# Regrouping the columns of the modulations' weight pieces: four 128-column matmuls a piece

## The chip, the cores and the metric

The kernel runs on one core of one Trainium2 chip. The metric is the device time of one execution in microseconds, taken as the median of several runs. Beside the times there is one profiled execution of the kernel before; its page and its trace are what the numbers below are read from.

## The reference

The program is two transformer-like blocks in float32, with 256 latent tokens, 256 context tokens and 1024 features. The first block has two layers; each layer's input is modulated by a shift, a scale and a gate that come from a condition vector, once for the latents (`c`) and once for the context (`c_ctx`):

```python
cond = jax.nn.silu(c)
cond_ctx = jax.nn.silu(c_ctx)
for i in range(DEPTH):
    sh, sc, gt = jnp.split(cond @ w_mod[i] + b_mod[i], 3, axis=-1)
    sh_c, sc_c, gt_c = jnp.split(cond_ctx @ w_mod[i] + b_mod[i], 3, axis=-1)
    h_lat = x * (1.0 + sc[:, None]) + sh[:, None]
    h_ctx = ctx * (1.0 + sc_c) + sh_c
    ...
    x = _layernorm(DEEPNORM_ALPHA * x + gt[:, None] * y_lat, ln_g[i], ln_b[i])
```

`w_mod[i]` is 1024 x 3072. Layer 0 is an attention with 16 heads (MLA), layer 1 a state space mixer (S5). The second block has a pooling and gating mixer, a cross attention and a feed-forward part. The products `cond @ w_mod[i]` and `cond_ctx @ w_mod[i]` are what the change is about.

## The kernel before

TensorE multiplies the transposed weights of a piece with activations that stand with features on the partitions. Most products are written as three matmuls of rounded parts (L119, L120, L121: high by high, high by low, low by high). The modulations are different: the condition, only two columns wide and padded to 32 (`self.cs`), is the stationary operand, and the raw float32 weights are the moving one. Such a matmul fills 32 of the array's 128 columns, one of its four column groups, and writes 32 partitions of the bank `modps`. A float32 matmul leaves two records in the trace, so four records are two matmuls.

Layer 0's shift and scale are computed at the very start (`start`, L678): four matmuls of 128 columns in the four column groups, for eight chunks of features, four rounds from each 1 MB piece. The rest goes through `mod` (from L577): layer 0's gate (part 1, 1024 columns), then layer 1's shift and scale (part 0, 2048 columns) and its gate (part 1). Each part has 1024 rows in eight chunks `kc`, and pieces `mraw` of 512 columns (256 KB, two buffers), loaded by SyncE at L588. The bank's partitions 32 j to 32 j + 31 hold the j-th quarter of the part's columns: `w` is 512 columns for part 0 and 256 for part 1. So a piece of part 0 is one matmul of 512 columns in one group, and a piece of part 1 two matmuls of 256 columns in two groups. There are 16 + 32 + 16 = 64 pieces. After a part ScalarE copies the bank out (L596), TensorE turns it (L601), and VectorE adds the bias (L604).

`mod` is a generator. Each call of `side` takes one step of it, a piece or an end, and some steps of the S5 operators' preparation (`s5_prep`: sp_t, sp_r, sp_o on VectorE, rtps and gps on TensorE). `side` is called once after each of 16 gate chunks (`mla_in`) and three times in each of the 18 rounds of the heads' pipeline (`mla_heads`): after the value projection of two heads back (uv), after the next head's `values` (pv), and after `queries` (qabs), ahead of `turn` (ptl, ptc). What is left is run before layer 0's norm (`ln_mod`).

TensorE keeps the order in which the code is written. On VectorE, ScalarE and SyncE a scheduler decides, by its own estimate of when things are ready; so a change in TensorE's work can shift the order on these engines, too. SyncE's queue is strict: a reload of `mraw` that waits for a buffer holds up what stands behind it.

Of the kernel before, what the change touches and what calls it, by code (L numbers as in the profile page):

```python
# [11 lines left out]
F32 = mybir.dt.float32  # L12
# [16 lines left out]
class InOrder:  # L29
    """An engine whose instructions go through net.in_order."""  # L30
# [9 lines left out]
class Net:  # L40
# [16 lines left out]
    def phase(self, wts, **banks):  # L57
        """A phase's weight pieces (raw and as parts: numbers of buffers) and its share-out of PSUM's eight banks."""
# [9 lines left out]
    def pinned(self, *engines):  # L68
        """Instructions of these engines, too, keep the order that they are written in."""
# [5 lines left out]
    @contextmanager  # L75
    def behind(self, level=1):
        """What is written in this context fills the gaps of what is written outside."""
        self.tc.cur_priority += 1000000 * level
        yield
        self.tc.cur_priority -= 1000000 * level  # L80
# [7 lines left out]
    def weight(self, src, keep=None):  # L88
        """A weight piece [128, 1024] from DRAM as its parts (high, low); keep: a pool, a name and a number of
        buffers for those that are used more than once."""  # L90
# [20 lines left out]
    def in_order(self, ins):  # L111
        """Keeps an instruction behind those that are written before it, where its engine is in self.ordered."""
# [3 lines left out]
    def mm(self, out, a, b, start, stop):  # L116
        """out += a.T @ b, with a and b given as (high, low)."""
# [6 lines left out]
    def rms_open(self, n, nk, feats, tp, bufs=2, tag="ps", cut=0):  # L124
        """Sums up the squares of nk chunks [128, n], over the chunks first and then over the partitions: one column
        of the bank per 128 tokens. Chunk cut starts a second sum over chunks."""
# [13 lines left out]
    def rms_sum(self, r):  # L140
        """The sum over the partitions, of every n-th column."""
# [7 lines left out]
    def rsqrt(self, s, y, scale, tp):  # L149
        """y = 1 / sqrt(s * scale + eps): the exponent's half, negated, and three Newton steps."""  # L150
# [9 lines left out]
    def rms_close(self, r, between=None, tag="ps"):  # L160
        """1 / sqrt(mean + eps) of each token, on every partition [128, n], in PSUM."""
# [23 lines left out]
    def s5_lambda(self, lam, pool, tp):  # L185
        """Powers of lambda-bar, the input coefficient and the scan's multipliers, from lam and log_dt; in steps."""
        nc, v = self.nc, InOrder(self, self.nc.vector)
        n = 128
# [56 lines left out]
        # powers: [128, re/im, dir*pair, 9]  # L245
# [26 lines left out]
        # (lambda-bar - 1) / lam  # L272
# [17 lines left out]
        # powers 1..8, and 0..7 times that coefficient: per direction and piece (re, re + im, im - re) of [j, power]  # L290
# [1495 lines left out]
```

## Time and profile before

| | |
|---|---|
| median of three runs | 1501.27 us (1500.88 to 1508.71) |
| span of the profiled execution, first to last instruction | 1494.4 us |
| TensorE busy | 1379.3 us, 92% |
| VectorE busy | 1152.3 us, 77% |
| ScalarE busy | 712.5 us, 48% |

The profiled execution's own time is its span of 1494.4 us and what lies around it. The page does not give the latter; the median of the runs is 6.9 us above the span. A piece's matmuls overlap with their neighbours, and the ends of matmuls are modelled, so the distance from one start to the next says more than a record's own duration.

### The profile page before, as it was taken

The numbers are of one execution on the slowest core, as the hardware profiler recorded it, in microseconds if no ns is written. First come the engines' busy times: TensorE is split into PE (matmuls) and PEld (weight loads), VectorE is DVE, ScalarE is ACT, GpSimd is POOL, SyncE is SP. The second block draws the span as 40 slices with busy tenths as digits, with TensorE's granted clock in tenths as the row PEclk, the third lists the DMA queues.
The fourth block names the chain that finished last, engine by engine and source line by source line (L and its number), as shares of the span: only waits on it lengthen the run. The fifth ranks groups of instructions, "written<-read, shape, count | busy, mean of one in ns | idle before, by whom it ended". The sixth has DMA issues, their size and how long they took to land.

```text
span 1494.4 us, 30436 instructions
## 1 busy us (share of the span) xinstructions
PE 1379.3 (92%) x12192; PEld 1201.1 (80%) x12192; DVE 1152.3 (77%) x2122; ACT 712.5 (48%) x1307; POOL 100.5 (7%) x221
## 2 busy tenths in 40 slices
PE   5889979999999998898877779999998999999997
PEld 4657656667777778798866669999998999999996
DVE  7989886787768779839988966755568876788887
ACT  4434435655555544622244244544447556565554
POOL 0012211110011011001111000000000000000000
PEclk9989988999999999999988989999999999999999
DMA  9459984454435444578787676555555544445552
GB/s 359 160 170 319 297 247 127 141 156 143 140 120 156 149 131 139 174 223 282 276 294 281 246 266 212 194 194 198 184 183 164 171 169 141 158 171 192 187 184 99
DMA packets 140622, 291.35 MB, mean 195 GB/s; under 512 B 30480, under 2 KB 70080, under 8 KB 135104
## 3 DMA queue, kind: packets, MB, share of 16 engines
q1 hardware_dynamic: 108592, 232.01, 45.5%
q0 software_dynamic: 11360, 49.34, 10.4%
q10 hardware_dynamic: 20528, 8.06, 2.0%
q8 instruction: 95, 1.56, 0.4%
q14 instruction: 47, 0.39, 0.1%
HBM read 234.83 MB, written 54.53 MB: 194 GB/s over the span
## 4 chain that ended last, share of the span: by engine, by line
PE 69%; DVE 15%; issue 7%; DMA 6%; ACT 2%; POOL 0%; SPq 0%; DVEq 0%; ACTq 0%; POOLq 0%
PE lin L119 14%; PE lin L120 14%; PE lin L121 13%; PE modps L591 3%; DVE s_t L493 3%; DVE wl L98 2%; DMA sp_x<-in_s_bcw_dram 2%; PE slat L119 2%; DMA d_o<-sp_o 1%; PE sctx L119 1%; PE dn L121 1%; PE dn L119 1%; PE dn L120 1%; DVE s_V L495 1%; DVE sp_t L37 1%
## 5 line engine op out<-in xcount | busy, mean ns | idle before, releaser
L97 ACT CAST wh<-wr 128x1024 fp32r<-128x1024 f32 x268 | 280.5, 1048 | 407.2 <-PE lin L120 250.0
L98 DVE TENSOR_TENSOR wl<-wr,wh 128x1024 fp32r<-128x1024 f32 x268 | 327.5, 1223 | 148.2 <-ACT wh L97 147.7
L119 PE MATMUL lin<-prH,wh 128*128 128x256 f32 x512 | 145.3, 284 | 0.0
L119 PE MATMUL lin<-yaH,wh 128*128 128x256 f32 x512 | 144.8, 283 | 0.0
L120 PE MATMUL lin<-yaL,wh 128*128 128x256 f32 x512 | 144.6, 282 | 0.0
L121 PE MATMUL lin<-prH,wl 128*128 128x256 f32 x512 | 143.7, 281 | 1.0 <-DVE wl L98 1.0
L121 PE MATMUL lin<-yaH,wl 128*128 128x256 f32 x512 | 144.1, 281 | 0.0
L120 PE MATMUL lin<-prL,wh 128*128 128x256 f32 x512 | 143.8, 281 | 0.2 <-DVE prL L109 0.2
L120 PEld LDWEIGHTS lin<-prL,wh 128*128 128x128 f32 x512 | 96.7, 189 | 1.7 <-DVE prL L109 0.6
L119 PEld LDWEIGHTS lin<-yaH,wh 128*128 128x128 f32 x512 | 97.5, 190 | 0.0
L119 PEld LDWEIGHTS lin<-prH,wh 128*128 128x128 f32 x512 | 96.7, 189 | 1.0
L121 PEld LDWEIGHTS lin<-yaH,wl 128*128 128x128 f32 x512 | 97.4, 190 | 0.0
L120 PEld LDWEIGHTS lin<-yaL,wh 128*128 128x128 f32 x512 | 97.3, 190 | 0.0
L121 PEld LDWEIGHTS lin<-prH,wl 128*128 128x128 f32 x512 | 96.3, 188 | 1.2 <-DVE wl L98 1.2
L493 DVE TENSOR_TENSOR s_t<-s_V,s_tab 128x256 f32<-128x256 f32 (+2 forms) x120 | 73.2, 652 | 15.7 <-ACT s_V L475 14.5
L121 PE MATMUL u<-h,wl 128*128 128x256 f32 x224 | 66.0, 295 | 9.3 <-DVE wl L98 9.3
L427 POOL DMA_DIRECT2D d_t<-sp_g x128 | 66.8, 529 | 56.9 <-DVE sp_g L37 52.6
L121 PE MATMUL lin<-h,wl 128*128 128x256 f32 x128 | 42.4, 331 | 29.7 <-DVE wl L98 29.7
L119 PE MATMUL u<-h,wh 128*128 128x256 f32 x224 | 66.1, 295 | 0.0
L120 PE MATMUL u<-h,wh 128*128 128x256 f32 x224 | 65.6, 293 | 0.5 <-issue 0.5
L119 PE MATMUL lin<-hH,wh 128*128 128x512 f32 x144 | 60.6, 421 | 0.7 <-ACT hH L103 0.7
L37 DVE TENSOR_TENSOR sp_t<-s_pb,sp_x 128x1024 f32<-128x1024 f32 x64 | 60.0, 952 | 0.6
(481 smaller groups left out, 3871.8 us busy)
## 6 DMA issues: line engine op xcount, KB each, us to landing
wr<-in_glu_dram SPq DMA_DIRECT2D x64, 512.0 KB, 3.3
wr<-in_w_up_dram SPq DMA_DIRECT2D x44, 512.0 KB, 4.2
wr<-in_w_in_dram SPq DMA_DIRECT2D x32, 512.0 KB, 4.8
mraw<-in_w_mod_dram SPq DMA_DIRECT2D x64, 256.0 KB, 3.1
d_rt<-sp_rt SPq DMA_DIRECT2D x64, 256.0 KB, 4.0
d_o<-sp_o SPq DMA_DIRECT2D x32, 512.0 KB, 4.8
wr<-in_s_in_dram SPq DMA_DIRECT2D x32, 512.0 KB, 4.5
s_op<-d_o POOLq DMA_DIRECT2D x16, 1024.0 KB, 7.9
```

What stands on the lines that cost most here:

```text
L37: return lambda *a, **k: self.net.in_order(f(*a, **k))
L97: self.in_order(nc.scalar.copy(hi, raw))
L98: self.in_order(nc.vector.tensor_tensor(lo, raw, hi.bitcast(F32), SUB))
L119: self.in_order(t.matmul(out, a[0], b[0], start=start, stop=False))
L120: self.in_order(t.matmul(out, a[0], b[1], start=False, stop=False))
L121: self.in_order(t.matmul(out, a[1], b[0], start=False, stop=stop))
L427: nc.gpsimd.dma_start(self.d_t[k].rearrange("s i j e c -> i s j e c")[:, :, j, e], a)
L493: go(v.tensor_tensor(t[:, x], src.to_broadcast([128, 2, 32, n]), a[x].unsqueeze(1).to_broadcast([128, 2, 32, n]), MUL))
L495: go(v.tensor_tensor(dst, dst, t[:, 0], ADD))
L591: self.in_order(nc.tensor.matmul(p[32 * j:32 * j + 32, :w], self.cs[:, kc, :], raw[:, jj * w:jj * w + w], start=(kc == 0), stop=(kc == 7), ...
```

## The change

The host lays each part's weights out as [kc, q, 128 rows, 4 groups, 128 columns]. Piece q of a chunk then holds 128 columns of each of the four quarters, as one contiguous stretch of 256 KB, and its four matmuls of 128 columns go to the four column groups, at columns 128 q of the bank. The number of pieces, their size, the bank's final content, and the steps between which `side` divides the work stay. The clearing flag is now given with the first piece of a part alone (`kc` 0 and `q` 0), once for each group, and the last flag with the last piece. The copy for the start of layer 0 is made from the same array on the host. Comments and docstrings are dropped, too, which changes nothing in the program.

```diff
-    def mod(self, i, parts, m, tp, piece=512, bufs=2):
+    def mod(self, i, parts, m, tp):
         nc = self.nc
         for part in parts:
             src = self.I[f"w_mod{i}_{part}"]
-            w = 512 if part == 0 else 256
+            n = src.shape[1]
             p = self.ps("modps")
             for kc in range(8):
-                for q in range(4 * w // piece):
-                    raw = tp.tile([128, piece], F32, name="mraw", bufs=bufs)
-                    nc.sync.dma_start(raw, src[kc, :, q * piece:q * piece + piece])
-                    for jj in range(piece // w):
-                        j = q * (piece // w) + jj
+                for q in range(n):
+                    raw = tp.tile([128, 4, 128], F32, name="mraw", bufs=2)
+                    nc.sync.dma_start(raw, src[kc, q])
+                    for j in range(4):
                         self.in_order(nc.tensor.matmul(
-                            p[32 * j:32 * j + 32, :w], self.cs[:, kc, :], raw[:, jj * w:jj * w + w],
-                            start=(kc == 0), stop=(kc == 7), skip_group_check=True))
+                            p[32 * j:32 * j + 32, q * 128:q * 128 + 128], self.cs[:, kc, :], raw[:, j],
+                            start=(kc == 0 and q == 0), stop=(kc == 7 and q == n - 1), skip_group_check=True))
                     yield
+            w = 128 * n
             row = tp.tile([128, 512], F32, name="sp_rt", bufs=2)[:, :w]
...
-            n = w // 128
...
-            o[f"w_mod{n}_{k}"] = f(w[n, :, :, c])
-    w = o.pop("w_mod0_0").reshape(2, 4, 128, 2, 4, 256)
+            o[f"w_mod{n}_{k}"] = f(w[n, :, :, c].reshape(8, 128, 4, -1, 128).transpose(0, 3, 1, 2, 4))
+    w = w[0, :, :, 0:2048].reshape(2, 4, 128, 2, 4, 256)
+    del o["w_mod0_0"]
```

On TensorE, in the first round of the heads, between a head's queries (qabs) and the turning of its probabilities (ptl, ptc), there stands before:

```order
L120 MATMUL qabs<-qnL,waH 128x512
L121 MATMUL qabs<-qnH,waL 128x512
L591 MATMUL modps<-mraw,cs 32x512
L866 MATMUL ptl<-ident,P 128x128 x8
L873 MATMUL ptc<-ident,P 128x128 x4
L119 MATMUL slat<-ckH,qaH 128x512
```

and now:

```order
L120 MATMUL qabs<-qnL,waH 128x512
L121 MATMUL qabs<-qnH,waL 128x512
L591 MATMUL modps<-mraw,cs 32x128 x4
L866 MATMUL ptl<-ident,P 128x128 x8
L873 MATMUL ptc<-ident,P 128x128 x4
L119 MATMUL slat<-ckH,qaH 128x512
```

Nothing moved there; the one matmul has become four. TensorE's order is otherwise the same everywhere.

On VectorE, at the same place (qaL is the low part of the queries that `slat` reads next, sp_t a step of the S5 operators, ptlL and ptcL the low parts of the turned probabilities), there stands before:

```order
L37 TENSOR_TENSOR sp_t_2491<-s_pw,sp_x 128x1024
L37 SCALAR_TENSOR_TENSOR sp_g<-dmask,dskip,sp_g 128x16 x2
L104 TENSOR_TENSOR qaL<-qabs,qaH 128x512
L104 TENSOR_TENSOR ptlL<-ptl,ptlH 128x4x128 x2
L104 TENSOR_TENSOR ptcL<-ptc,ptcH 128x512
L649 TENSOR_REDUCE sm_st<-slat 128x1 x2
L37 TENSOR_TENSOR sp_t_2492<-s_pw,sp_x 128x512
```

and now:

```order
L37 TENSOR_TENSOR sp_t_2535<-s_pw,sp_x 128x1024
L37 SCALAR_TENSOR_TENSOR sp_g<-dmask,dskip,sp_g 128x16 x2
L37 TENSOR_TENSOR sp_t_2536<-s_pw,sp_x 128x512
L104 TENSOR_TENSOR qaL<-qabs,qaH 128x512
L104 TENSOR_TENSOR ptlL<-ptl,ptlH 128x4x128 x2
L104 TENSOR_TENSOR ptcL<-ptc,ptcH 128x512
L649 TENSOR_REDUCE sm_st<-slat 128x1 x2
```

The 512-element step sp_t has moved ahead of qaL. Such moves by a place or two are found in VectorE's and ScalarE's order up to the end of the heads, none behind.

On SyncE's queue, in the ninth round of the heads (sgl is a head's gate, read by VectorE after uv; d_o and d_rt are the S5 operators on their way to scratch), there stands before:

```order
L393 DMA d_o<-sp_o 128x8x128
L588 DMA mraw<-in_w_mod_0_dram 128x512
L84 DMA sgl<-d_sg 128x512
L588 DMA mraw<-in_w_mod_0_dram 128x512 x2
L405 DMA d_rt<-sp_rt 128x512 x2
```

and now:

```order
L393 DMA d_o<-sp_o 128x8x128
L589 DMA mraw<-in_w_mod_0_dram 128x512 x2
L84 DMA sgl<-d_sg 128x512
L589 DMA mraw<-in_w_mod_0_dram 128x512
L405 DMA d_rt<-sp_rt 128x512 x2
```

One reload more stands ahead of sgl.

## Rows read from the trace of the kernel before

**Rows 1.** Page: busy time by engine, and the chain's shares by engine.

```profile
PE 1379.3 (92%) x12192; PEld 1201.1 (80%) x12192; DVE 1152.3 (77%) x2122; ACT 712.5 (48%) x1307; POOL 100.5 (7%) x221
...
PE 69%; DVE 15%; issue 7%; DMA 6%; ACT 2%; POOL 0%; SPq 0%; DVEq 0%; ACTq 0%; POOLq 0%
```

**Rows 2.** Chain from 100 to 205 us; a TensorE wait from 55 to 205 us.

```profile
by line: DMA sp_x<-in_s_bcw_dram 23.5%; DMA d_o<-sp_o 20.3%; issue 18.6%; DVE sp_t L37 11.9%; DVE sp_r L37 10.1%; DVE sp_o L37 8.8%; DVE wl L98 2.7%; DVE sp_g L37 1.9%; DVEq L37 0.9%; ACT sp_o L390 0.9%; DVE sp_x L37 0.3%; ACT sp_x L357 0.3
...
PE gps L413 <- DVE sp_o L37: 7.5, 7, 1.9
```

**Rows 3.** Windows: stretch, length; busy PE, PEld, DVE, ACT, POOL (count); PEclk, DMA.

```profile
229.60:555.00 325.40, 325.40 (x2147) 233.33 (x2147) 248.65 (x455) 177.83 (x390) 30.77 (x70) 0.99 0.46 141
...
229.60:323.70 94.10, 94.10 (x637) 63.28 (x636) 72.61 (x139) 57.33 (x133) 9.07 (x22) 0.98 0.47 140
```

**Rows 4.** Chain from 230 to 555 us, shares by engine and line.

```profile
by line: PE modps L591 12.3%; PE slat L119 7.0%; PE lin L119 6.9%; PE lin L120 6.2%; PE lin L121 6.1%; PE sctx L119 5.8%; PE ptl L866 5.0%; PE rtps L400 4.7%; PE slat L120 4.3%; PE slat L121 4.3%; PE pv L119 4.2%; PE pv L120 3.5%; PE pv L12
```

**Rows 5.** L591's groups by shape; a window of modps alone (PE, PEld, ACT).

```profile
L591 PE MATMUL modps<-mraw,cs 128*32 128x512 f32 x64 | 33.3, 633 | 0.0
...
L591 PE MATMUL modps<-mraw,cs 128*32 128x256 f32 x128 | 20.0, 391 | 0.0
...
440.00:555.00 115.00, 10.01 (x64) 2.31 (x64) 0.37 (x1) 1.00 0.45 140
```

**Rows 6.** Chain: the first two pieces, and their window; timeline of TensorE: two others.

```profile
229.62 1.85 PE modps L591 x4
...
229.60:231.40 1.80, 1.80 (x5) 0.14 (x4) 0.87 (x4) 1.56 (x5) 0.00 (x0) 0.50 0.00 0
...
268.94 1.05 PE L591 MATMUL modps<-mraw,cs 128*32 128x512 f32 x2
269.92 1.09 PE L400 MATMUL rtps<-ident,sp_r 128*128 128x128 f32 x8
...
492.30 0.63 PE L591 MATMUL modps<-mraw,cs 128*32 128x256 f32 x4
492.85 0.51 PE L119 MATMUL qrope<-qnH,wh 128*128 128x512 f32 x1
```

**Rows 7.** Timeline of TensorE around L678 (start us, us, ...; in brackets idle time before).

```profile
17.54 1.87 PE L678 MATMUL modps<-mraw,cs 128*32 128x128 f32 x32 [0.45 <-DMA mraw<-in_w_mod_dram]
19.34 0.50 PE L119 MATMUL lin<-hH,wh 128*128 128x512 f32 x1
...
34.73 1.08 PE L678 MATMUL modps<-mraw,cs 128*32 128x128 f32 x32 [0.77 <-DMA mraw<-in_w_mod_dram]
35.74 0.50 PE L119 MATMUL lin<-hH,wh 128*128 128x512 f32 x1
```

**Rows 8.** Chain from 55 to 63 us: the first weight piece in it.

```profile
55.52 0.56 PE modps L591 x4
```

**Rows 9.** Page: the pieces' loads (median us to landing); timelines of SyncE and VectorE.

```profile
mraw<-in_w_mod_dram SPq DMA_DIRECT2D x64, 256.0 KB, 3.1
...
264.15 0.33 SPq L588 DMA_DIRECT2D mraw<-in_w_mod_dram  x1
...
386.39 5.61 SPq L588 DMA_DIRECT2D mraw<-in_w_mod_dram  x2
...
404.09 0.68 DVE L895 TENSOR_TENSOR sgl<-uv,sgl 128x512 f32<-128x512 f32 x1
```

**Rows 10.** VectorE's waits from 229.6 to 323.7 us: total us, times, longest.

```profile
DVE sp_r L37 <- PE gps L413: 4.4, 3, 2.9
...
DVE qfrL L104 <- ACT qfrH L103: 2.6, 2, 1.9
...
DVE oL L104 <- ACT oH L103: 0.3, 1, 0.3
```

**Rows 11.** Timelines of VectorE and TensorE: the tightest queries of the heads.

```profile
237.36 0.68 DVE L104 TENSOR_TENSOR qaL<-qabs,qaH 128x512 fp32r<-128x512 f32 x1
...
238.71 0.40 PE L121 MATMUL slat<-ckH,qaL 128*128 128x512 f32 x1
```

## The prediction

> **What bounds the kernel now.** I read the page first, then the windows by stage, then the chain and the waits inside the stage that the edit touches. TensorE is the engine to look at: it is busy 92% of the 1494.4 us span, VectorE 77%, and the chain that ended last is 69% TensorE [rows 1]. That is an average, so the stages decide. The modulations' 64 weight pieces are spread over two of them. From about 100 to 205 us, while the gates are computed, the chain runs through transfers (sp_x 23.5%, d_o 20.3%) and VectorE, and no weight-piece matmul is among the lines that lead its list [rows 2]. From 229.6 to 555 us, the sixteen heads, TensorE is busy 325.40 of 325.40 us, VectorE 248.65 and ScalarE 177.83 [rows 3]; the chain is TensorE's and "modps L591", the matmuls that the diff rewrites, is its largest line with 12.3%, some 40 us [rows 4]. So whatever TensorE time is taken out between 229.6 and 555 us should come off the end, and what is taken out before 205 us should not.
>
> **The pieces and their price today.** Part 0 of layer 1 has 32 pieces, each one 512-column matmul (64 records, two per matmul). The two 1024-column parts have 16 pieces each, each two 256-column matmuls in two column groups (128 records, half of them from 440 to 555 us, so the other half before the heads) [rows 5]. A price is the distance from the piece's first record to the start of the next matmul. The piece of 512 columns: 268.94 to 269.92, 0.98 us. The pair of 256: 492.30 to 492.85, 0.55 us. The first two 512-column pieces stand side by side at a granted clock of 0.50 (1.2 GHz): 1.85 us of the chain for both [rows 6]. So the pair, with the same 512 columns of weights, already gets most of what two groups can give.
>
> **The price after.** No row of the second stage shows four 128-column matmuls in four groups, but line L678 issues exactly that form at the start of the kernel, four rounds at a time: 32 records from 34.73 until the next matmul at 35.74, 1.01 us [rows 7]. From the two prices above, 256 columns more per matmul cost 0.98 - 0.55 = 0.43 us, so a piece is about 0.12 us of entering and leaving plus 0.00168 us a column; 128 columns give 0.12 + 0.215 = 0.335. The same formula gives 0.12 + 4 x 0.215 = 0.98 for the four rounds where the row has 1.01, so I take 0.34 us a piece. Bounds: below, 1.01 / 4 = 0.25, as if entry and exit cost a lone piece no more than their share; above, the other row of L678, the same 32 records in 1.80 us (17.54 to 19.34) [rows 7], which makes (1.80 - 0.12) / 4 + 0.12 = 0.54. The row at 34.73 is the nearer one, since its pace agrees with the formula, which comes from the heads.
>
> **The sum.** (a) Thirty 512-column pieces in the heads: 30 x (0.98 - 0.34) = 19.2 us. (b) The first two: two rounds of quads are 0.12 + 2 x 0.215 = 0.55 us at 2.4 GHz, twice that at 1.2 GHz, so 1.85 - 1.1 = 0.75, about 0.8 us. (c) Sixteen pairs in the heads: 16 x (0.55 - 0.34) = 3.4 us. (d) The sixteen pairs before 205 us: only the first two stand in the chain (the first at 55.52 with 0.56) [rows 8], 0.4 us; the others take TensorE time where TensorE waits for VectorE anyway (gps for sp_o, 7.5 us [rows 2]), and I cost them at nothing. If that cover were gone they would give 14 x 0.21 = 2.9 us more. Together 23.8 us.
>
> What the edit adds: 320 more matmul records and as many weight loads. They are in the 0.34, since the L678 row contains its weight loads. The transfers stay 64 of 256 KB, now each one contiguous stretch of memory; a piece's 2 KB rows stay 2 KB rows. They land in 3.1 us [rows 9], and nothing waits for them in the heads. Is that cover kept? Each of the two buffers is refilled when the matmuls of two pieces earlier end: such a load goes out at 264.15 [rows 9], lands 3.1 us later at about 267.3, and is read at 268.94 [rows 6]: 1.7 us to spare. After, the buffer is free 0.64 us sooner and wanted 1.28 us sooner, so about 1.1 us stay. This is the tightest kind, three pieces within one head, and I cost it at nothing; if the cover goes it is 0 to 1 us for each of some 16 heads. In SyncE's order a reload or two changes places with a neighbour. Where one now stands ahead of sgl, a head's gate, sgl goes out behind a wait for the next piece: that reload went out at 386.39, and this sgl is read at 404.09 [rows 9], so it has time enough behind it.
>
> **What is late next: VectorE.** With TensorE faster, VectorE has the same work in less time. The worst stretch is the first, 229.6 to 323.7 us: TensorE 94.1 us, VectorE busy 72.6 [rows 3]. TensorE loses 15 x 0.64 + 0.8 = 10.4 us there and would need 83.7. VectorE's idle time of 21.5 us is 8.9 of waiting for ScalarE (seven rows, from 2.6 to 0.3) and the rest nearly all of waiting for TensorE [rows 10]. The latter shrinks as TensorE gets faster, the former doesn't: 72.6 + 8.9 = 81.5, which is just under 83.7. So it fits, with little to spare, and not at every place: qaL, the low part of a head's queries, ends at 238.04 and the scores read it at 238.71 [rows 11], 0.67 us of slack, while one piece (0.64 us) goes from between and the new order puts a 0.68 us step of the background work ahead of it. Such places are few. Their price lies between 0 and the 10.4 us that the stretch could gain; I take 2.5 us, near the lower end because 81.5 still fits. In the rest of the heads VectorE is busy 248.65 - 72.61 = 176.0 of 231.3 us, and I take nothing.
>
> 23.8 - 2.5 = 21.3 us. The span of this profile would fall from 1494.4 to about 1473. The median of the runs, 1501.27, lies 6.9 us above the span, by what lies around it; I subtract from the median: **1480.0 us**.
>
> **Rivals.** *VectorE binds in the first five heads.* If all of its 21.5 us of waiting stays, that stretch gains nothing and 10.4 us of (a) and (b) are lost: 23.8 - 10.4 = 13.4, 1487.9 us. For it: 81.5 against 83.7, and VectorE's order mixes long background steps with what the scores need. Against: more than half of the waiting is for TensorE itself, and the background can slip, since it is mostly the S5 operators' steps (sp_t, sp_r, sp_o), which no score reads.
>
> *The instructions' rate binds.* Eight records a piece instead of two is the dear side of this edit. If a record costs what the 17.54 row says, the piece is 0.54 us: 30 x 0.44 + 16 x 0.01 = 13.4 us with nothing for (b) and (d), 1487.9 us. Against: the 34.73 row has 32 records in 1.01 us, 32 ns each, weight loads included. The Trainium skill speaks against the change here: "TensorE: Matmul & The Clock Gate", section "Wait — 56ns, not 53.3ns?", gives about 62 ns of the sequencer for each matmul when its hardware decoder is off. By that rule eight records would make an estimated 0.50 + 0.12 = 0.62 us a piece, the pairs would lose, and the gain would be about 10 us; the trace's 32 ns disagrees, and the measurement decides.
>
> *The four don't lie side by side.* This is the slower side. One record of 512 columns is (0.98 - 0.12) / 2 = 0.43 us, of 128 columns 0.107; eight in a row with the entry are 0.98 us. The 512-column pieces then gain nothing and each pair loses 0.43: 18 on the path, 7.7 us, 1509 us. It decides from 0.83 us a piece on, where 30 x 0.98 + 16 x 0.55 = 46 x 0.83. Against: L678's rows and the pair's own 0.55.
>
> *Nothing is left at the end*: the heads get shorter, and the norm after them, which runs on VectorE too, waits for background work that has been pushed back. Then 1497 to 1503 us. Against: that work has places of its own written after the heads, and VectorE would still have some 55 us of idle time in the heads (325.4 - 23 - 248.65).
>
> **How the numbers follow.** Forecast, 1476 to 1485 us: 0.66. More than that (0.25 us a piece, or no friction), 1472 to 1476: 0.08. VectorE binds, 1485 to 1488: 0.13. Instruction rate, 1487.9: 0.08. Nothing left: 0.03. Not side by side: 0.02. The range 1474 to 1488 us takes in the forecast, most of the two middle cases, and the better part of the good one. About 0.5%, 7.5 us, is what a measurement of this kernel can tell from no change: faster by over that 0.95, within it 0.03, slower 0.02.
>
> **What would show it.** In the changed profile: pieces at L591 as eight records with 0.33 to 0.36 us to the next matmul; "modps L591" in the heads' chain down from 40 to about 17 us; the heads' end at 532 to 535 instead of 555 us; TensorE with only a few waits for qaL, wl or mraw in it; the stage before 205 us where it was. I am wrong if L591's records follow each other at 50 ns or more, if TensorE waits for VectorE by more than 5 us between 229 and 320 us, if a piece waits for its load in most heads, or if the stretch after the heads gets longer by what the heads lost.

## The result: 22 us less, where the pieces stood

The changed kernel takes 1478.57 us in the median (1474.39 to 1479.44, four runs) against 1501.08 us before (four runs, too): a ratio of 0.9843, with a 95% interval from 0.9814 to 0.9872. The profiled execution took 1474.39 us with a span of 1472.6 us, 21.8 us less than the span before. The prediction was 1480.0 us, 21.3 us less.

The first lines of the page after answer to [rows 1] (busy time and count by engine, then the chain's shares):

```profile
PE 1356.5 (92%) x12512; PEld 1203.9 (82%) x12512; DVE 1150.7 (78%) x2122; ACT 712.6 (48%) x1307; POOL 100.5 (7%) x221
...
PE 67%; DVE 20%; DMA 6%; issue 3%; ACT 3%; SPq 0%; ACTq 0%; DVEq 0%
```

TensorE has 320 instructions more and is busy 22.8 us less. The other engines are as busy as they were, within 2 us. To see where the time goes, the same matmul is looked up in both traces. The heads begin with the first qabs (after a wait for its weights), and a matmul of the output projection, `lin<-vg,wh`, ends them. Timelines of TensorE (start, us), before:

```profile
214.35 0.79 PE L119 MATMUL qabs<-qnH,waH 128*128 128x512 f32 x1 [4.78 <-DMA wr<-in_w_out_dram]
...
557.73 0.39 PE L119 MATMUL lin<-vg,wh 128*128 128x512 f32 x1
```

and after:

```profile
213.91 0.80 PE L119 MATMUL qabs<-qnH,waH 128*128 128x512 f32 x1 [5.02 <-DMA wr<-in_w_out_dram]
...
536.53 0.39 PE L119 MATMUL lin<-vg,wh 128*128 128x512 f32 x1
```

Between these two matmuls lie 343.38 us before and 322.62 us after. So 20.76 us of the 21.8 are gained in the heads, 0.44 before them, and the rest behind them. Windows and chain of the heads after, for [rows 3] and [rows 4] (stretch, length, busy PE, PEld, DVE, ACT, POOL with counts, granted clock, DMA; then the chain's shares by line):

```profile
229.10:536.50 307.40, 306.42 (x2415) 236.78 (x2415) 249.91 (x460) 178.51 (x391) 30.77 (x70) 0.99 0.52 150
229.10:314.40 85.30, 84.51 (x739) 64.06 (x738) 71.58 (x138) 56.97 (x133) 8.90 (x21) 0.98 0.54 153
...
by line: PE lin L119 7.5%; PE slat L119 7.2%; PE lin L120 6.8%; PE lin L121 6.8%; PE sctx L119 6.1%; PE slat L121 4.8%; PE modps L591 4.6%; PE slat L120 4.3%; PE ptl L866 4.3%; PE rtps L400 4.0%; PE pv L119 3.9%; PE pv L120 3.3%; PE pv L121
```

"modps L591" went from the first place with 12.3% to the seventh with 4.6%, some 14 us. That is less than the "about 17" which the prediction named as a sign, because the chain of the heads now runs over VectorE for some 23 us, in the stretches that end with the waits for qaL below; the pieces themselves sum to 17.40 us (table below). TensorE is still busy for all but 1 us of this stretch. This is one head's stretch of TensorE's timeline after:

```profile
262.66 0.28 PE L121 MATMUL pv<-ptcH,ctL 128*128 128x256 f32 x1
262.87 0.43 PE L591 MATMUL modps<-mraw,cs 128*32 128x128 f32 x8
263.23 0.50 PE L119 MATMUL qabs<-qnH,waH 128*128 128x512 f32 x1
263.56 0.40 PE L120 MATMUL qabs<-qnL,waH 128*128 128x512 f32 x1
...
264.48 0.39 PE L121 MATMUL qabs<-qnH,waL 128*128 128x512 f32 x1
264.80 0.43 PE L591 MATMUL modps<-mraw,cs 128*32 128x128 f32 x8
265.15 0.55 PE L400 MATMUL rtps<-ident,sp_r 128*128 128x128 f32 x3
```

A piece is eight records, and the next matmul starts 0.36 us behind its first. All 46 single visits of the heads take 0.355 to 0.358 us. The two pieces side by side at the lower clock take 1.01 us (229.18 to 230.19) in place of 1.85. What is late now (TensorE's waits from 205 to 536.5 us: total, times, longest):

```profile
PE qabs L119 <- DMA wr<-in_w_out_dram: 5.0, 1, 5.0
PE slat L121 <- DVE qaL L104: 1.0, 3, 0.5
PE gps L413 <- DVE sp_o L37: 0.7, 1, 0.7
PE slat L119 <- ACT qaH L103: 0.7, 1, 0.7
PE qabs L121 <- DVE waL L104: 0.6, 1, 0.6
```

The second row is new: the scores wait three times for qaL. There is no row for mraw.

### The profile page after: what moved, and what is told of

Read it like the earlier page. It is cut to its first block, busy times and chain, and to the rows that moved or that the text cites. A ratio compares the mean times of both kernels' runs of the same rounds, so it can differ in the third digit from the quotient of the medians.

```text
span 1472.6 us, 31082 instructions
## 1 busy us (share of the span) xinstructions
PE 1356.5 (92%) x12512; PEld 1203.9 (82%) x12512; DVE 1150.7 (78%) x2122; ACT 712.6 (48%) x1307; POOL 100.5 (7%) x221
## 4 chain that ended last, share of the span: by engine, by line
PE 67%; DVE 20%; DMA 6%; issue 3%; ACT 3%; SPq 0%; ACTq 0%; DVEq 0%
PE lin L119 14%; PE lin L120 14%; PE lin L121 14%; DVE s_t L493 4%; DVE wl L98 3%; DMA sp_x<-in_s_bcw_dram 2%; DVE s_V L495 2%; DMA d_o<-sp_o 2%; PE slat L119 2%; DVE sp_t L37 2%; PE sctx L119 1%; PE dn L121 1%; PE dn L119 1%; PE dn L120 1%; PE vps L472 1%
```

## The experiments

Thirteen kernels stand beside the one before. This table collects what the sections below use. "Heads" is the distance between the two matmuls above. "Visits" is the time from the first record of each visit to the pieces until the next matmul, summed over the heads. Each ratio is to the kernel before, run on the same chip in the same hour; its median there was 1498.4 to 1501.1 us.

| kernel | heads, us | visits, us | median, us | ratio (95%) |
|---|---|---|---|---|
| before | 343.38 | 40.04 | 1501.08 | 1 |
| changed | 322.62 | 17.40 | 1478.57 | 0.9843 (0.9814 to 0.9872) |
| quads in part 0 only | 325.81 | 20.60 | 1479.38 | 0.9863 (0.9833 to 0.9893) |
| own groups | 343.79 | 41.42 | 1497.91 | 0.9991 (0.9974 to 1.0008) |
| one group | 347.68 | 44.07 | 1508.57 | 1.0064 (1.0040 to 1.0088) |
| pairs everywhere | 330.95 | 26.60 | 1484.75 | 0.9912 (0.9881 to 0.9944) |
| one chunk of eight | 301.42 | 2.44 | 1453.76 | 0.9710 (0.9677 to 0.9742) |
| short stretches | 322.62 | 17.40 | 1478.36 | 0.9860 (0.9843 to 0.9877) |
| one buffer | 339.90 | 20.61 | 1495.70 | 0.9976 (0.9958 to 0.9995) |
| queries first | 321.19 | 17.40 | 1475.84 | 0.9854 (0.9831 to 0.9877) |
| two rounds | 320.62 | 14.67 | 1474.50 | 0.9833 (0.9816 to 0.9850) |
| two rounds, queries first | 315.98 | 14.23 | 1473.27 | 0.9819 (0.9794 to 0.9845) |
| one, none, two | 318.03 | 15.26 | 1474.45 | 0.9837 (0.9807 to 0.9867) |
| the same, queries first | 318.08 | 15.26 | 1473.59 | 0.9820 (0.9792 to 0.9847) |

The medians and the spans hold some noise that the heads don't. The stage before the heads, which the transfers lead, began the heads between 1.4 us earlier and 5.1 us later than the kernel before, also in kernels whose TensorE work there hardly differs. So the heads' length is the finer measure here. It has some 0.6 us of its own: the granted clock is 0.50 when the heads begin, and the moment at which it rises differs from profile to profile. Of the eleven ranges of time that were expected of these runs, eight miss the median, by 0.6 to 3.3 us and once by 9.2; the sections below therefore go by the traces.

### Is it the lying side by side?

Two kernels keep eight records of 128 columns a piece and take the four groups away. The first has the old layout and gives each matmul of a piece to the group that its columns belonged to, one group for part 0 and two for part 1:

```diff
-                    nc.sync.dma_start(raw, src[kc, q])
-                    for j in range(4):
+                    nc.sync.dma_start(raw, src[kc, :, q * 512:q * 512 + 512].rearrange("p (a c) -> p a c", a=4))
+                    for cc in range(n):
+                        for jj in range(4 // n):
+                            j = q * (4 // n) + jj
...
```

> The old layout of the weights, but each piece as four 128-column matmuls: in part 0 all four in the piece's one column group, in the 1024-column parts two and two in its two groups. Theory (side by side is what saves): a part 0 piece has eight records one after another, 0.107 us each, 0.98 to 1.0 us, as much as the one matmul before; a pair stays at 0.55 to 0.58 us. Time of the kernel before, 1500 to 1504 us. Rival (smaller matmuls are cheaper as such, because entry and end overlap better): a piece falls below 0.8 us and the time to 1495 us or less.

It ran in 1497.91 us, ratio 0.9991. Its timeline shows a piece of part 0, then one of part 1:

```profile
238.47 1.06 PE L593 MATMUL modps<-mraw,cs 128*32 128x128 f32 x8
239.46 0.33 PE L868 MATMUL ptl<-ident,P 128*128 128x128 f32 x1
...
495.23 0.63 PE L593 MATMUL modps<-mraw,cs 128*32 128x128 f32 x8
495.79 0.50 PE L119 MATMUL qrope<-qnH,wh 128*128 128x512 f32 x1
```

Eight records in one group take 0.99 us (0.98 for two records of 512 columns before), in two groups 0.56 (0.55 before), in four 0.36. So in these pieces the number of records costs 0.015 us at most, and the number of groups is the whole difference. One place differs: the first two pieces, which stand back to back in two different groups at the lower clock, take 2.71 us in place of 1.85. With eight records each, their starts show the two side by side for a part of the time only; why is not shown.

The second sends all four to the first group, from the second chunk of features on, and keeps everything else of the changed kernel but the last flag, which goes with the last matmul alone:

```diff
-                            p[32 * j:32 * j + 32, q * 128:q * 128 + 128], ...
+                            p[(0 if kc else 32 * j):(0 if kc else 32 * j) + 32, q * 128:q * 128 + 128], ...
```

> The changed kernel, but from the second chunk of features on, all four matmuls of a piece go to the first column group (so the sums of the three other quarters are left out from there, and the first group sums all of them). The instructions, the weights' loads, the layout and the steps are the changed kernel's; only the lying side by side is taken away. It is the prediction's third rival, made. Theory (side by side is the whole of the gain): eight records of 128 columns in one group take 0.99 us, as a 512-column piece in the run with the matmuls in their own group, also where a pair of 256 columns took 0.556. In the heads: the first two pieces 1.01 us at the lower clock, four quads 0.356, 42 pieces 0.99, in sum 44.0 us against 40.0 before and 17.4 in the changed kernel: the heads about 4 us longer than before, 26 us longer than changed; median 1503 to 1507 us. Rival (part of the gain comes from the layout, the shorter instructions or the clearing flags): the heads stay shorter than before, under 1498 us.

It ran in 1508.57 us, ratio 1.0064 (1.0040 to 1.0088). A piece in its timeline:

```profile
269.85 1.06 PE L591 MATMUL modps<-mraw,cs 128*32 128x128 f32 x8
270.84 0.50 PE L119 MATMUL qabs<-qnH,waH 128*128 128x512 f32 x1
```

The visits sum to 44.07 us where the theory had 44.0, and the heads are 4.30 us longer than before. That is the prediction's third rival, with its price (0.99 us a piece, where it had 0.98) and its sign: the change without the four groups makes the kernel slower. In this profile the heads also begin 5.07 us later than before, and its median is 10 us up, more than the heads give; TensorE's pieces before 205 us took 19.2 us in place of 13.2 there. Whether those 6 us reached the end or the stage was late by itself, one profile can't tell.

### Part by part

Quads for part 0 alone, with part 1 as pairs of 256 columns as before:

```diff
             for kc in range(8):
+                if part == 1:
+                    for q in range(2):
+                        raw = tp.tile([128, 512], F32, name="mraw", bufs=2)
+                        nc.sync.dma_start(raw, src[kc, :, q * 512:q * 512 + 512])
+                        ...
```

> Part 0 of layer 1 (32 pieces of 512 columns) gets the new layout and four matmuls a piece; the two 1024-column parts keep two matmuls of 256 columns in two groups. Theory (TensorE binds in the heads, a piece costs what its records and its entry cost): 30 x (0.98 - 0.36) + 0.8 = 19.4 us less in the heads, 1 to 2 of it lost to waits; 1482 to 1484 us, and the pieces of the gates' stage change nothing that can be seen. Rival (the gain comes from the loads' new layout or from the moved order on the other engines): these apply to all 64 pieces, so half of the layouts gives half of the gain, about 1490 us.

It ran in 1479.38 us, ratio 0.9863. The heads are 17.57 us shorter than before, the changed kernel's 20.76. So the sixteen pieces of part 1 in the heads are worth 3.2 us, which is 16 x (0.556 - 0.356).

Pairs everywhere: a piece of part 0 is two matmuls of 256 columns in two groups, too.

```diff
-                    raw = tp.tile([128, 4, 128], F32, name="mraw", bufs=2)
+                    raw = tp.tile([128, 2, 256], F32, name="mraw", bufs=2)
...
-                    for j in range(4):
+                    for jj in range(2):
+                        j, c = q % 2 * 2 + jj, q // 2 * 256
...
```

> Every piece, also of part 0, as two 256-column matmuls in two column groups. Theory (0.12 to 0.14 us of entry and end and 0.00168 us a column): a part 0 piece at 0.55 us, 30 x 0.42 + 0.75 = 13.4 us less in the heads, about 1 us of it lost to waits: 1488 to 1490 us. Rival (two groups already give all that TensorE's clock or the loads allow): about as fast as the changed kernel, 1479 to 1482 us.

It ran in 1484.75 us, ratio 0.9912. The heads are 12.43 us shorter. The visits' sum fell by 40.04 - 26.60 = 13.4, and from the first piece on the queries took 0.54 us more and the scores 0.24. The queries' share lies in the heads' first round and is the clock's, not VectorE's: TensorE is busy throughout, and its granted clock is 0.50 (window, columns as above), where the kernel before had 1.00 at the same matmuls.

```profile
232.82:234.00 1.18, 1.18 (x11) 0.99 (x4) 0.92 (x3) 0.12 (x1) 0.11 (x1) 0.50 1.04 380
```

Two groups bring 60% of what four do.

### What a visit really costs

Here seven of the eight chunks of features are left out, with their loads, while the steps stay:

```diff
                 for q in range(n):
+                    if kc:
+                        yield
+                        continue
...
```

> The changed kernel with the first of the eight chunks of features alone in mod (the loads and matmuls of the other seven are left out, so the modulations are sums over 128 features; the steps stay). Theory (TensorE alone still binds in the heads after the change): 42 pieces of 0.36 us fewer there, 15 us less than the changed kernel, 1463 to 1465 us, with TensorE's waits below 3 us from 229 us to the heads' end. Rival (VectorE is the bound right behind, most of all in the first five heads): 1467 to 1474 us, with waits of TensorE for VectorE of 4 us and more there.

It ran in 1453.76 us, ratio 0.9710, and so some 10 us faster than the theory's figure. Most of that stands in the heads: 301.42 us, 41.96 less than before and 21.20 less than the changed kernel. The 42 visits left out account for 17.40 - 2.44 = 14.96 us by their own price. Where the rest is shows when the same place is read without a visit. This kernel's timeline, for the rows at 262.66 to 265.15 above:

```profile
261.82 0.28 PE L121 MATMUL pv<-ptcH,ctL 128*128 128x256 f32 x1
261.93 0.39 PE L119 MATMUL qabs<-qnH,waH 128*128 128x512 f32 x1
262.17 0.40 PE L120 MATMUL qabs<-qnL,waH 128*128 128x512 f32 x1
...
263.09 0.40 PE L121 MATMUL qabs<-qnH,waL 128*128 128x512 f32 x1
263.32 1.03 PE L400 MATMUL rtps<-ident,sp_r 128*128 128x128 f32 x8
```

Without a visit the last pv is followed 0.11 us later, with one 0.21. The first qabs is followed after 0.24, and 0.33 behind a visit. The last qabs takes 0.23, and 0.32 ahead of one. So the neighbours pay 0.15 to 0.20 us for a visit that the price "until the next matmul" doesn't hold. Over the 42 visits left out, the matmuls ahead sum to 3.76 us more in the changed kernel, and those behind to 3.47: 0.17 us a visit. In all, from the first visit to the end of the heads, TensorE's other matmuls took 5.75 us more there than here, 0.64 of it in the scores that wait for VectorE; the sum is smaller than its parts because this kernel has waits for VectorE of its own (1.6 us in all, some at places where the changed kernel doesn't wait). This part was the same before the change and is still there after it. It cancels in the difference, and that is why the prediction came out right without it.

If that is so, fewer visits with more in them must pay. Two pieces at a time, in every second step, from one 512 KB buffer:

```diff
-                for q in range(n):
-                    raw = tp.tile([128, 4, 128], F32, name="mraw", bufs=2)
-                    nc.sync.dma_start(raw, src[kc, q])
+                for q in range(0, n, 2):
+                    raw = tp.tile([128, 2, 4, 128], F32, name="mraw", bufs=1)
+                    nc.sync.dma_start(raw, src[kc, q:q + 2].rearrange("q p j c -> p q j c"))
...
                     yield
+                    yield
```

> The quads as changed, but two pieces at a time: one load of 512 KB (one buffer of it in place of two of 256 KB) and two rounds of quads in every second step; the other step has none. It tells apart where the price of a piece lies. In the trace of the changed kernel a piece takes 0.356 us until the next matmul, and beside the same matmuls without a piece its two neighbours are longer, too: 0.09 us the one ahead, 0.06 to 0.11 the one behind. Theory 1, the neighbours' part is the cost of changing between the whole array and its column groups, and is paid once per visit: two rounds take 0.356 + 0.218 = 0.57 us, 0.14 less than two pieces, and 0.15 to 0.20 us of the neighbours goes as well; with 23 visits fewer in the heads 6.7 to 7.8 us, so about 7 us under the changed kernel, 1471 to 1473 us, ratio to before about 0.980. Theory 2, the neighbours' part belongs to the columns themselves and doubles with them: 23 x 0.14 = 3.2 us, 1475 us. Theory 3, VectorE has no more room: the gain turns into TensorE's waits for qaL and others, under 2 us in all, 1477 us or more. The one load may also come late (about 4.5 us to land, with 10 us and more between visits): no wait expected.

It ran in 1474.50 us, ratio 0.9833. The price of a visit is as the first theory has it (timeline):

```profile
265.11 0.64 PE L592 MATMUL modps<-mraw,cs 128*32 128x128 f32 x16
265.69 1.09 PE L400 MATMUL rtps<-ident,sp_r 128*128 128x128 f32 x8
```

0.575 us for two rounds, so a second round adds 0.22 us. But the heads are only 2.0 us shorter than the changed kernel's, not 7. Most of what is missing lies at one place. Timelines of TensorE and VectorE, and windows around it (stretch, length, busy PE, PEld, DVE, ACT, POOL, granted clock, DMA):

```profile
283.74 0.40 PE L120 MATMUL slat<-ckL,qaH 128*128 128x512 f32 x1
285.44 0.50 PE L121 MATMUL slat<-ckH,qaL 128*128 128x512 f32 x1 [1.30 <-DVE qaL L104]
...
283.23 1.22 DVE L98 TENSOR_TENSOR wl<-wr,wh 128x1024 fp32r<-128x1024 f32 x1
...
284.70 0.68 DVE L104 TENSOR_TENSOR qaL<-qabs,qaH 128x512 fp32r<-128x512 f32 x1
...
284.00:287.50 3.50, 2.20 (x11) 1.44 (x10) 3.50 (x7) 0.88 (x2) 0.00 (x0) 1.00 0.60 193
287.50:298.00 10.50, 10.50 (x79) 7.56 (x77) 3.94 (x9) 6.25 (x15) 0.00 (x0) 0.53 0.15 51
298.00:310.00 12.00, 12.00 (x100) 9.39 (x85) 10.42 (x18) 5.53 (x12) 0.11 (x1) 0.99 0.63 191
```

No piece stands between that head's queries and its scores any more, a weight piece's wl (1.22 us) stands ahead of qaL on VectorE, and TensorE waits 1.30 us. Two microseconds later its granted clock is 0.53, that is 1.2 GHz in nearly all of the stretch, for 10.5 us. At the higher clock the work of those 10.5 us takes about half, so the clock cost an estimated 5 us and the wait 1.3. That the wait brought the clock down is likely, but not shown.

The same with the split of the queries ahead of the background's steps on VectorE:

```diff
-            self.split(*qa, p)
+            self.tc.cur_priority -= 2000000; self.split(*qa, p); self.tc.cur_priority += 2000000
```

> Two pieces at a time in every second step (as in the run of two rounds) and the priority for the queries' split. In the run of two rounds the visits cost what its first theory says, 0.575 us and the neighbours' share once, but the gain went: at 285 us qaL stood behind a weight piece's wl on VectorE, TensorE waited 1.3 us for it, and its granted clock was 0.53 from 287.5 to 298 us, some 5 us lost in that stretch. Theory (the loss is that one wait and the clock behind it): with the priority qaL stands ahead of sp_t in the first round, but at 285 us wl still stands ahead of it, since wl is ready sooner; so if the wait stays, the time stays at 1473 to 1475 us; if the shifted order happens to take it away, 1468 to 1470 us. Rival: VectorE is short of time in general, and with fewer waits at one place others come: 1473 us or more, with the clock high.

It ran in 1473.27 us (1470.69 to 1476.44), ratio 0.9819 (0.9794 to 0.9845). The windows of the same stretches (same columns), and TensorE's waits from 222 to 540 us:

```profile
284.00:287.50 3.50, 3.01 (x20) 2.31 (x18) 3.50 (x8) 2.20 (x5) 0.00 (x0) 1.00 0.72 216
287.50:298.00 10.50, 10.02 (x100) 7.59 (x101) 7.82 (x16) 6.27 (x17) 0.11 (x1) 1.00 0.34 113
...
PE slat L121 <- DVE qaL L104: 1.5, 2, 1.0
PE slat L119 <- ACT qaH L103: 0.7, 1, 0.7
```

The heads begin 2.75 us later in this profile, so the wait at that head now falls around 287.5 us. It is still there, 1.0 us, but the clock stays at 1.00. That is neither of the theory's two cases: the wait stayed, and the clock behind it did not fall. By its time alone the run would fit the rival, too; but the heads are 4.6 us shorter than without the priority, and that the rival doesn't have. The heads are 315.98 us, 6.64 us shorter than the changed kernel's: 3.17 us in the visits' own price, and 3.79 in the neighbours (the scores wait 0.29 us more). With 23 visits less, that is 0.14 us inside and 0.165 outside for each. So the neighbours' part is paid by the visit and not by the column. Of the kernels that leave nothing out this has the shortest heads and the lowest median, and it beats the one before; against the changed kernel the medians are 5.3 us apart, but the intervals of the two ratios still overlap.

A third share-out, one piece after the value projection and two after the queries, was to give every head's qaL more cover:

```diff
+            for k in range(8 * n):
+                c = min((1, 0, 2)[k % 3] if k < 8 * n - 1 else 2, 8 * n - t)
...
```

> The changed kernel's quads with another share-out over the three steps of a head's round: one piece after the value projection, none after the values, two pieces at once after the queries, from one buffer of 512 KB. Every head's queries then have 0.575 us of pieces (in place of 0.356) between them and the scores, and a head has two visits in place of three. By the rows: 0.14 us inside and 0.15 to 0.20 us of the neighbours saved for about 15 heads is 4.4 to 5.1 us, and the 1.8 us of waits for qaL in the changed kernel go for the larger part, since each gets 0.22 us more of cover and needs 0.07 to 0.68: about 6 us under the changed kernel, 1471 to 1473 us. Rival 1 (VectorE is at its limit in the first five heads, as the run of two rounds seemed to say): the saved time turns into waits there and the clock falls behind them: 1476 us or more. Rival 2: the load of two pieces, which can only go out when the one piece is multiplied, comes late at the queries (about 5 to 6 us for 4.0 us): waits for mraw in some heads, 0 to 1 us each, 1474 to 1480 us.

It ran in 1474.45 us, ratio 0.9837. The heads are 318.03 us, 4.6 less than the changed kernel's, as the visits and the neighbours give; the waits for qaL did not go (1.1 us in two). The longest, 0.9 us, is now in the round where a 1024-column sp_t stands ahead of qaL; the changed kernel waited 0.19 us there. Its loads made no wait in the heads.

> The share-out of one, none and two pieces, and the priority for the queries' split on VectorE. Against the run without the priority: if VectorE's order is what is left of the waits for qaL, up to 0.7 us less; if there are none left by the longer cover, the same within 0.3 us in the trace. About 1470 to 1473 us. Rival: the other order makes background steps late, and TensorE waits for them (gps, rtps) in the heads: slower than without by 1 us or more.

With the queries first as well: 1473.59 us, heads 318.08. The scores gained 0.65 us, as the first case of the expectation has it. But 0.55 us came back in the queries of the heads' first round, which ran at the lower granted clock (window, columns as above), where the run without the priority had 1.00 at the same matmuls:

```profile
236.05:237.07 1.02, 1.02 (x10) 0.83 (x3) 0.79 (x3) 0.00 (x0) 0.11 (x1) 0.50 0.89 343
```

Whether the priority moved the clock's rise or it came later by itself isn't shown, so the equal heads don't tell what the priority is worth. The rival (background steps late by over 1 us) did not come.

### VectorE and the loads

The split of the queries first, in the changed kernel, alone:

> The changed kernel, with one thing more: the split of a head's queries (qaH, qaL) has a priority over the background's steps in the scheduler's order. TensorE's order stays. On VectorE qaL stands again ahead of the 512-column sp_t in the heads' first round, as in the kernel before; nothing moves in the two other rounds where TensorE waits for qaL (283 and 315 us), since a 1024-column sp_t is ready there before qaL is. In the trace of the changed kernel the low scores of the first round come 0.68 us late, of the two others 0.44 and 0.47. Theory: these waits are VectorE's order alone, and all of what the heads lost: the first goes, the others stay, the heads end 0.6 to 0.7 us sooner (about 1478 us). Rival: VectorE has no room, and what sp_t loses there TensorE waits for elsewhere (rtps or gps late by the same 0.6 us): the heads end where they did. The difference is seen in the trace, not in the median.

In the changed kernel VectorE's timeline in the first round has a step ahead of qaL that nobody there waits for:

```profile
234.77 1.23 DVE L37 TENSOR_TENSOR sp_t<-s_pw,sp_x 128x1024 f32<-128x1024 f32 x1
235.91 0.38 DVE L37 SCALAR_TENSOR_TENSOR sp_g<-dmask,dskip,sp_g 128x16 f32<-128x16 f32 x2
236.21 0.68 DVE L37 TENSOR_TENSOR sp_t<-s_pw,sp_x 128x512 f32<-128x512 f32 x1
236.81 0.68 DVE L104 TENSOR_TENSOR qaL<-qabs,qaH 128x512 fp32r<-128x512 f32 x1
```

and TensorE's low scores started at 237.55, 0.91 us behind the ones ahead of them, where 0.23 is usual. With the priority (VectorE's timeline, then TensorE's waits from 222 to 545 us):

```profile
235.02 1.23 DVE L37 TENSOR_TENSOR sp_t<-s_pw,sp_x 128x1024 f32<-128x1024 f32 x1
236.16 0.69 DVE L104 TENSOR_TENSOR qaL<-qabs,qaH 128x512 fp32r<-128x512 f32 x1
...
PE slat L121 <- DVE qaL L104: 0.5, 2, 0.3
```

This wait is gone and the two others stay, as expected; nothing else got later. The heads are 321.19 us, 1.4 us shorter, of which the scores are 0.83; another 0.6 us is rtps and gps at the heads' start, where the granted clock, 0.50 until then, rose sooner (0.75 in place of 0.66 from 231 to 234 us). The median of 1475.84 us can't carry this difference.

One buffer for the pieces in place of two (`bufs=1`):

> The changed kernel with one buffer for the pieces in place of two: a load goes out only when the piece before it has been multiplied. It tells whether the loads, costed at nothing, are hidden by a margin or by much. By the trace of the changed kernel the visits of a head lie about 5 to 8, 2 to 2.7 and 5 to 10 us apart, and a load lands in 3.2 us after a start that is about 0.1 us behind the release. Theory (margin near 1.1 us, tightest between the second and the third visit of a head): one wait in most heads, 0.6 to 1.3 us each, 10 to 18 us in all, so 1489 to 1497 us, and TensorE's waits for mraw stand in the heads' list with 10 to 16 times. Rival: the loads are far from mattering (there is other work to hide behind), 1479 to 1482 us.

It ran in 1495.70 us, ratio 0.9976: the change's gain is nearly gone. The longest of TensorE's waits from 222 to 545 us:

```profile
PE modps L591 <- DMA mraw<-in_w_mod_dram: 13.8, 11, 3.0
```

A load took 2.8 us here, and in eleven places it came late. So it is the second buffer that hides the loads; with it the tightest piece still has 1.42 us to spare, as worked out below.

The old layout in memory, from which a load gathers 512-byte stretches:

```diff
-                    nc.sync.dma_start(raw, src[kc, q])
+                    nc.sync.dma_start(raw, src[kc].rearrange("p (j q c) -> p q j c", j=4, q=n)[:, q])
```

> The changed kernel's matmuls, but with the weights laid out in memory as before: a load then gathers 512-byte stretches, four to a row, in place of one contiguous 256 KB. It tells whether the layout in memory is part of the gain. Theory (the gain is TensorE's and the loads have 1.4 us to spare): a load lands in 3.2 to 4.5 us, the matmuls cost what they do, 1478 to 1482 us, with waits for mraw in some heads if it is over 4.5 us. Rival (short stretches cost the transfers much more, or they disturb the gates' stage before 205 us, where the chain runs through transfers): 1484 to 1495 us, with waits for mraw in the heads or a later end of the gates' stage.

It ran in 1478.36 us, ratio 0.9860, with visits that sum to 17.40 us and heads of 322.62 us, both as in the changed kernel. That the heads agree to the hundredth is chance: the first round's queries took 0.6 us more at the lower clock, and the scores took 0.6 us less, since they wait for qaL in two places and not in three. The page's row of its loads (KB each, median us to landing):

```profile
mraw<-in_w_mod_dram SPq DMA_DIRECT2D x64, 256.0 KB, 3.3
```

3.3 us in place of 3.2. The contiguous layout is no part of the gain, nor needed for it.

## Why the prediction held, point by point

**The bound.** Right. TensorE is busy 306.42 of 307.40 us in the heads after the change, and what was taken from it there came off the end: 20.76 us in the heads, 21.8 in the span. The matmul that ended the heads moved from 557.73 to 536.53.

**The price of a piece.** Forecast 0.34 us from the 512-column and the 256-column prices and L678's row at 34.73; measured 0.356. No visit in the heads took what the row at 17.54 would make, 0.54. The trace of the kernel before shows what that row most likely was. Another row of L678, at 25.82, needs 1.72 us for the same 32 records, and there the granted clock is low (timeline, then windows over both rows):

```profile
25.82 1.79 PE L678 MATMUL modps<-mraw,cs 128*32 128x128 f32 x32 [1.32 <-DMA mraw<-in_w_mod_dram]
...
25.82:27.54 1.72, 1.72 (x32) 1.34 (x32) 1.05 (x2) 1.72 (x5) 0.00 (x0) 0.56 1.07 332
17.54:19.34 1.80, 1.80 (x33) 1.39 (x33) 1.66 (x6) 0.82 (x2) 0.00 (x0) 1.00 1.09 379
```

The window over 17.54 shows 1.00, but the first entry on the clock in this trace is at 19.21 us, and a window without an entry shows 1.00. So 1.80 us is most likely a price at the lower clock. If so, the upper bound of 0.54 and the rival of the instructions' rate, which is built on it, had no row of the higher clock behind them.

**The terms.** (a) 30 x (0.976 - 0.356) = 18.6 us for 19.2. (b) 1.853 - 1.013 = 0.84 for 0.8. (c) 16 x 0.20 = 3.2 for 3.4; the kernel with part 0 alone shows it directly as 3.2. Together 22.64 us, which is the difference of the visits' sums, for 23.4. (d) The 0.4 us before 205 us can't be confirmed: the heads began 0.44 us sooner, but in the other kernels that start moved by itself, from 1.4 us earlier to 5.1 us later than before.

**VectorE.** Forecast 2.5 us; measured 1.81, all of it in the scores (from the first piece on slat took 55.34 us in place of 53.53, all other matmuls the same within 0.03). The place was the one named: qaL in the first round, 0.68 us late behind the moved sp_t, and two more. The run with the queries first shows the cause for the first of the three. For the other two (0.44 and 0.47 us, behind a 1024-column sp_t) the timelines show what stands ahead, but no run moved it. The stretch that took 94.1 us before takes 85.3 (229.10 to 314.40), for the 83.7 that TensorE was to need without any wait. 22.64 - 1.81 = 20.83, against 20.76 measured.

**The loads.** At least 1.1 us to spare was forecast; the smallest margin in the trace is 1.42 us, at the piece of 264.80, whose load went out at 260.66. No piece waits in the heads.

**The rivals.** VectorE didn't bind: with most pieces left out, the heads still shrink to 301.42 us, with VectorE's work in them as before and 1.6 us of waits for it. Its idle time in the first stretch fell from 21.5 us to 85.30 - 71.58 = 13.7. The rate of instructions didn't bind: eight records take 0.356 us, 0.56 or 0.99, by the groups they go to. The Trainium skill's 62 ns a matmul with the hardware decoder off ("TensorE: Matmul & The Clock Gate", section "Wait — 56ns, not 53.3ns?"), which would have made an estimated 0.62 us a piece, is not what the runs show, in which it takes 0.356. Whether the decoder was on, no run tells. The third rival, made in the kernel with one group, costs 4.3 us in the heads with seven eighths of the pieces; the prediction had 7.7 us for all of them.

**From the span to the median.** The prediction put the 6.9 us between the span before and the median down to what lies around the span. The changed kernel's profiled execution has 1474.39 us and a span of 1472.61, so only 1.8 us lie around it; most of the 6.9 is then probably that the profiled execution before was faster than the median. It changed nothing, since the gain was taken off the median.

**What the prediction didn't see** is the neighbours' 0.15 to 0.20 us a visit. Its "0.12 us of entering and leaving" is only the part that lies before the next matmul. It changed no term, since the number of visits stayed.

## What to carry to other kernels

Price an operation that only changes its form by the distance to the next start, since what it costs its neighbours cancels; when it is added, removed or merged, look at the neighbours' distances with and without it as well. A matmul that fills 32 of the array's columns should have others for the remaining groups right behind it, and such small work should come in few visits rather than in many. Where TensorE is full and an operation between a producer and its reader gets shorter, the next wait can be the split that the reader needs; look at its place in VectorE's order first, and not at VectorE's load alone.

## What the runs showed of the hardware beyond that

- Four 128-column float32 matmuls of 32 rows of output in the four groups cost a further round of 0.219 us, as much as one alone in one group ((0.991 - 0.12) / 4 = 0.218, with the prediction's 0.12 for entry and exit). The Trainium skill has the same for other shapes: a packed set takes one matmul's duration and about 4 ns for each further one ("TensorE: Matmul & The Clock Gate", section "Measured speedup vs the span model"). By that a round would be an estimated 0.218 + 3 x 0.004 = 0.23 us, which the measured 0.219 is close to. Against the price of the same columns in one group the lone piece gains 0.991 / 0.356 = 2.8, not 4, because of the 0.14 us that a visit has beside its columns.
- A visit to the column groups lengthens the whole-array matmul ahead of it by 0.09 us and the one behind by 0.06 to 0.11 us, at the higher clock (42 visits of the changed kernel against the same places in the kernel with one chunk).
- One wait of 1.30 us in an otherwise full stretch was followed by 10.5 us at a granted clock of 0.53, some 5 us lost; a wait of 1.0 us at the same place left it at 1.00. What else the two differ in, the runs don't settle.
